# The maximum pass of an attention stage: two row tiles of the matrix array at a time, one maximum over two banks, and the maxima turned by one product and a DMA

## The chip, the cores and the metric

One Trainium2 chip, one of its cores. The metric is the device time of one launch in microseconds (us), the median of several runs. The engines are named as the profile names them: PE (matrix products; PEld its weight loads), DVE (vector), ACT (scalar), POOL (GpSimd) and SP (which issues most DMAs).

## The reference

Two layers over 1024 latent tokens and 256 context tokens of width 1024. Each layer projects the modulated stream once and splits the result into three groups of heads: six heads of a two-directional RWKV-7 recurrence, six attention heads with two key heads between them (grouped queries), and four heads of neighbourhood attention with a bias by relative position. The gated branches go through one output projection and a layer norm. The change touches the two attention branches, in the reference:

```python
def one_block(qi):                                # grouped-query heads, 128 queries at a time
    s = jnp.einsum('bqgrd,bsgd->bgrqs', qi, keys).astype(jnp.float32)
    p = jax.nn.softmax(s, axis=-1).astype(vals.dtype)
    return jnp.einsum('bgrqs,bsgd->bqgrd', p, vals)
...
s_nb = jnp.einsum('bqhd,bpqjhd->bhqpj', q_r, k_nb).astype(jnp.float32) + bias   # neighbourhood heads
s_ctx = jnp.einsum('bqhd,bchd->bhqc', q_r, k_ctx).astype(jnp.float32)
s = jnp.concatenate([s_nb.reshape(B, H, GRID_W, n_nb), s_ctx], axis=-1)
p = jax.nn.softmax(s, axis=-1).astype(v.dtype)
```

Queries and keys are 64 wide, and everything is float32. A softmax needs a value near each row's maximum taken off before the exponential; any value near it gives the same result.

## The kernel before

**Stages.** A layer is a projection, then the recurrence (`rwkv`) and the attention (`attention`), then the output projection (`out_proj`). The program is written in that order, but a scheduler sets each engine's order from a simulated time line, so the recurrence and the attention run mixed: in the profile the two share the stretches from about 560 to 1180 us (layer 0) and from about 1800 to 2390 us (layer 1). Each engine then works through its own fixed list and stops at the first instruction whose input is not there.

**Heads.** `heads` gives one piece of work after another, each of two "jobs" (two halves of its queries). A neighbourhood head (`na`) has 1024 queries and, per 128 queries, up to 384 neighbouring keys and 256 context keys. A grouped-query head (`all`) has 1024 queries on all 1280 keys. In layer 0 each of the ten heads also has a small piece for the context's own 256 queries (`ctx`). So there are 12 `all`, 8 `na` and 10 `ctx` pieces, 30 in the two layers. The loop at the end of `attention` runs the main pass of one piece (`pair_main`) with the maximum pass of the next (`pair_max`) between its steps.

**Operands.** A score is computed from float32 values split in a rounded high part and the rest (both `F32R`). `load_q` and `load_k` bring a head's queries and keys in twice, on partitions 0 to 63 and 64 to 127, and make two operands of each:

- first operand of q: high part, and rest below it; first operand of k: high part in both halves;
- second operand of q (65 rows): high part, and in row 64 the negated row maximum; second operand of k: rest, and a row of ones (L835).

Two products into one bank then give a score with its maximum taken off: L920 on the first operands, L921 on the second. ACT takes the exponential (L927), and L909 multiplies it with the values (tile `y`, in float32, which the profile shows as two passes of the array each, on 64 of its 128 columns).

**Maximum pass.** For each 128 queries, L863 multiplies the first operands into a bank `sm` (two such buffers), 512 keys at most at a time; DVE takes the maximum along the bank (L865; L867 adds the bias of a neighbourhood head as well), and L870 takes the maximum of these and negates it. When all queries of a piece are done, L876 turns each column of 128 maxima into a row by a product with the identity (one product for each 128 queries, on partition 64), and ACT copies a job's row into row 64 of the second query operand (L877). Only then can the piece's first L921 run.

In the names below `k_24741`, `q1_25626` and the like are buffers; `sm`, `st`, `y`, `ls`, `mt` are tiles in the accumulation memory: maximum pass, scores, output, sums of the softmax, turned maxima. `ch`, `kt`, `gt`, `mg` belong to the recurrence, `pso` to its output.

## Time and profile before

| what | value |
|---|---|
| three runs of the kernel | 2516.71, 2518.14, 2518.36 us (median 2518.14) |
| profiled execution, first to last instruction | 2517.7 us |
| busy: PE, DVE, POOL, ACT | 91%, 66%, 47%, 39% |
| maximum pass on PE: L863 | 436 products: 192 of 512 keys, 48 of 384, 196 of 256 |
| maxima turned: L876 | 360 passes (180 products in float32) |
| row maxima on DVE: L865, L867, L870 | 372, 64 and 180 instructions |

The profiled execution lasts as long as the runs: its span lies within 1 us of all three, so whatever its launch adds around the span is smaller than that, and a sum made against the span can be set beside the median as it is. A busy PE is not a PE at its peak: matrix products are pipelined, one begins before the other has ended, and the profile's durations of neighbours overlap. What a product costs is the distance from the end of one to the end of the next.

### The profile page before, as it was taken

What the parts mean: (1) busy time and instruction counts of PE and PEld (TensorE: products, weight loads), DVE (VectorE), ACT (ScalarE), POOL (GpSimd) and SP (SyncE); (2) the same over time, 40 slices, a digit from 0 to 9 for tenths busy, and PEclk for the clock granted to TensorE, in tenths of its full rate; (3) what the DMA queues carried; (4) which work ended last, traced back from release to release, by engine and by line L of the source; (5) the groups of instructions that cost most, each with busy time, mean ns of one, the idle gap of its engine ahead of it and who ended that gap; (6) DMA issues with size and microseconds to landing.
All of it is one profiled execution on the core that took longest, in us unless ns stands there. A gap on an engine that the chain in (4) does not pass through costs nothing. (4 is left out here: it accounts for less than half of the span.)

```text
span 2517.7 us, 56578 instructions
## 1 busy us (share of the span) xinstructions
PE 2289.5 (91%) x22008; PEld 1601.3 (64%) x22008; DVE 1669.4 (66%) x3183; ACT 979.5 (39%) x2074; POOL 1188.4 (47%) x1438
## 2 busy tenths in 40 slices
PE   6989999978898999999899999999778889999887
PEld 3878798765455554544887777887555554544387
DVE  5685524647878878665387885445478797786646
ACT  3433413333544444444233444133344444454422
POOL 4454425344555544453355465344455545544443
PEclk9999999997889999999999999999789898999999
DMA  7355325455555444441332546245645443332332
GB/s 276 117 167 169 106 80 137 101 139 115 123 117 124 104 109 102 114 140 54 104 98 95 159 143 199 87 97 138 154 105 123 101 96 97 83 80 64 112 110 95
DMA packets 448236, 298.09 MB, mean 118 GB/s; under 512 B 249600, under 2 KB 395880, under 8 KB 446944
## 3 DMA queue, kind: packets, MB, share of 16 engines
q1 hardware_dynamic: 439936, 281.71, 41.0%
q0 software_dynamic: 7392, 10.28, 1.5%
q8 instruction: 173, 2.83, 0.5%
q10 hardware_dynamic: 640, 2.49, 0.4%
q14 instruction: 95, 0.78, 0.1%
HBM read 198.37 MB, written 91.79 MB: 115 GB/s over the span
## 5 line engine op out<-in xcount | busy, mean ns | idle before, releaser
L204 PE MATMUL pj<-hlo,wh 128*128 128x512 f32 (+1 forms) x1072 | 400.7, 374 | 14.0 <-DVE hlo L480 7.9
L203 PE MATMUL pj<-hhi,wh 128*128 128x512 f32 (+1 forms) x1072 | 402.9, 377 | 9.8 <-ACT qr L348 5.9
L205 PE MATMUL pj<-hhi,wl 128*128 128x512 f32 (+1 forms) x1072 | 398.9, 373 | 0.2 <-POOL wl L169 0.2
L909 PE MATMUL y<-pt,v 128*64 128x512 f32 (+3 forms) x784 | 343.6, 570 | 0.0
L865 DVE TENSOR_REDUCE mx<-sm 128x1 f32<-128x512 f32 (+1 forms) x372 | 200.5, 555 | 85.4 <-PE sm L863 83.3
L169 POOL TENSOR_TENSOR wl<-wf,wh 128x512 fp32r<-128x512 f32 x104 | 142.9, 1378 | 205.8 <-ACT wh L168 181.8
L204 PEld LDWEIGHTS pj<-hlo,wh 128*128 128x128 f32 x1072 | 204.2, 191 | 55.3 <-DVE hlo L480 8.2
L203 PEld LDWEIGHTS pj<-hhi,wh 128*128 128x128 f32 x1072 | 203.9, 191 | 55.5 <-ACT qr L348 7.2
L927 ACT ACTIVATE pt<-st 128x512 f32<-128x512 f32 (+1 forms) x292 | 166.7, 583 | 179.4 <-PE st L921 176.9
L205 PEld LDWEIGHTS pj<-hhi,wl 128*128 128x128 f32 x1072 | 204.0, 190 | 37.2 <-issue 2.9
L863 PE MATMUL sm<-k,q 128*128 128x256 f32 (+2 forms) x436 | 167.2, 427 | 20.8 <-DVE mx L865 13.6
L920 PE MATMUL st<-q,k 128*128 128x512 f32 (+3 forms) x376 | 166.8, 447 | 18.3 <-DVE pt L929 6.2
L863 PEld LDWEIGHTS sm<-k,q 128*128 128x128 f32 x436 | 80.3, 203 | 151.8 <-DVE mx L865 41.6
L1141 PE MATMUL pj<-yh,wh 128*128 128x256 f32 x576 | 161.2, 291 | 15.9 <-ACT yh L1115 11.8
L934 POOL TENSOR_TENSOR acc<-acc,pt 128x512 f32<-128x512 f32 x80 | 107.0, 1337 | 138.1 <-ACT pt L927 137.6
L1142 PE MATMUL pj<-yl,wh 128*128 128x256 f32 x576 | 164.4, 288 | 1.0 <-POOL yl L1116 0.9
L1143 PE MATMUL pj<-yh,wl 128*128 128x256 f32 x576 | 162.8, 287 | 0.0
L921 PE MATMUL st<-q,k 65*128 65x512 f32 (+3 forms) x376 | 147.7, 396 | 1.8 <-issue 1.1
L909 PEld LDWEIGHTS y<-pt,v 128*64 128x64 f32 x784 | 72.0, 143 | 104.8 <-issue 94.1
L616 DVE TENSOR_TENSOR G<-gt,msk 64x192 f32<-64x192 f32 (+1 forms) x320 | 110.3, 345 | 39.4 <-PE gt L611 28.0
L920 PEld LDWEIGHTS st<-q,k 128*128 128x128 f32 x376 | 74.8, 200 | 93.8 <-ACT pt L927 28.1
L699 POOL MEMSET X<- 32x192 f32 x320 | 81.7, 255 | 108.8 <-PE ch L742 84.5
(276 smaller groups left out, 5126.5 us busy)
## 6 DMA issues: line engine op xcount, KB each, us to landing
wf<-win SPq DMA_DIRECT2D x104, 256.0 KB
wm<-wmod SPq DMA_DIRECT2D x32, 512.0 KB
yf<-yg_d SPq DMA_DIRECT2D x72, 128.0 KB
wt<-wm SPq DMA_DIRECT2D x8, 1024.0 KB
gate_d<-o SPq DMA_DIRECT2D x32, 256.0 KB
wf<-wout SPq DMA_DIRECT2D x16, 512.0 KB
ldkk<-rw_d SPq DMA_DIRECT2D x40, 192.0 KB
ldkd<-rw_d SPq DMA_DIRECT2D x40, 192.0 KB
```

Of the source, the lines that this page charges most:

```text
L203: nc.tensor.matmul(out=ps[:, :n], lhsT=wh, rhs=hhi[:, k, t0:t0 + n], start=(k == 0), stop=False)
L204: nc.tensor.matmul(out=ps[:, :n], lhsT=wh, rhs=hlo[:, k, t0:t0 + n], start=False, stop=False)
L205: nc.tensor.matmul(out=ps[:, :n], lhsT=wl, rhs=hhi[:, k, t0:t0 + n], start=False, stop=(k == KT - 1))
L863: nc.tensor.matmul(out=sp_[:, :o], lhsT=q[0][:, qc:qc + 128], rhs=k[0][:, c0:c0 + o], start=True, stop=True)
L865: nc.vector.tensor_reduce(out=mx[:, n_:n_ + 1], in_=sp_[:, :o], op=ALU.max, axis=AX.X)
L909: nc.tensor.matmul(out=o, lhsT=v[:, t, :], rhs=p_, start=start, stop=stop and n_ >= len(mm) - 2, tile_position=(0, 64 * i))
L920: nc.tensor.matmul(out=o, lhsT=k[0][:, 128 * t:128 * t + 128], rhs=q[0][:, qa:qb], start=True, stop=False)
L921: nc.tensor.matmul(out=o, lhsT=k[1][0:65, 128 * t:128 * t + 128], rhs=q[1][0:65, qa:qb], start=False, stop=True)
L927: nc.scalar.activation(out=pt[:, :w], in_=sp_[:, :w], func=AF.Exp)
L1141: nc.tensor.matmul(out=p_, lhsT=wh[m][:, k], rhs=yh, start=(x_ == 0), stop=False)
L1142: nc.tensor.matmul(out=p_, lhsT=wh[m][:, k], rhs=yl, start=False, stop=False)
L1143: nc.tensor.matmul(out=p_, lhsT=wl[m][:, k], rhs=yh, start=False, stop=(x_ == KT - 1))
```

## The change

What it does, part by part:

- **Operands laid out anew.** The first query operand holds the high part in both halves, the first key operand the high part with the rest below it. The second operands are four buffers of 128 partitions that stay for the whole layer (`kq0` to `kq3`): in q, the negated maximum in row 0, zeros, and the rest in rows 64 to 127; in k, a row of ones, zeros, and the high part in rows 64 to 127. Zeros and ones are written once a layer, by six DVE instructions. The second score product is 128 rows deep in place of 65.
- **Two row tiles at a time.** A product of the maximum pass is now 64 rows deep (high part by high part). Two of them are issued one behind the other, one on rows 0 to 63 of the array and one on rows 64 to 127, into two banks of one tile `sm`. That tile has one buffer, in a pool of its own, where there were two buffers of one bank.
- **One maximum over two banks.** For an `all` piece DVE takes the maximum over 1024 keys at once, and over the last 256 keys of two groups of queries at once; for a `ctx` piece over both groups. A neighbourhood head keeps its two reductions for each 128 queries. The last maximum, with the negation, is one instruction for a whole piece.
- **Turned by one product, flattened by a DMA.** One product with the identity turns all of a piece's maxima (up to 8 rows of 128), ACT copies them to a small tile `mr`, and a DMA that POOL issues lays the rows behind one another in row 0 of the second query operand.
- `load_k` has one more ACT copy, `load_q` one less.

The core of the diff:

```diff
+        psm = es.enter_context(tc.tile_pool(name=f"psm{l}", bufs=1, space=PSUM, side="right"))
...
+        kq2 = [ap1.tile([128, T], F32R, tag=f"kq{i}", name=f"kq{i}") for i in range(4)]
+        zsrc = ident[0:64, 0:64]
...
+        for z in kq2:
+            nc.vector.tensor_scalar(out=z[0:64, :], in0=zsrc[:, :].unsqueeze(2).to_broadcast([64, 64, 20]), scalar1=0.0, scalar2=None, op0=ALU.mult)
+        for z in kq2[0:2]:
+            nc.vector.tensor_scalar(out=z[0:1, :], in0=zsrc[0:1, :].unsqueeze(2).to_broadcast([1, 64, 20]), scalar1=0.0, scalar2=1.0, op0=ALU.mult, op1=ALU.add)
...
         def load_k(h):
...
-            k2 = ap2.tile([65, T], F32R, tag="k2", name="k2")
+            k2 = kq2[nkq[0] % 2]
             nc.scalar.copy(k1, sg_)
-            nc.gpsimd.tensor_tensor(out=k2[0:64, :], in0=sg_[0:64, :], in1=k1[0:64, :], op=ALU.subtract)
-            nc.vector.tensor_scalar(out=k2[64:65, :], in0=sg_[64:65, :], scalar1=0.0, scalar2=1.0, op0=ALU.mult, op1=ALU.add)
+            nc.scalar.copy(k2[64:128, :], k1[64:128, :])
+            nc.gpsimd.tensor_tensor(out=k1[64:128, :], in0=sg_[64:128, :], in1=k1[64:128, :], op=ALU.subtract)
...
         def load_q(h):
...
             nc.scalar.copy(q1[:, lo:], sg_[:, lo:])
-            nc.scalar.copy(q2[0:64, lo:], q1[0:64, lo:])
-            nc.gpsimd.tensor_tensor(out=q1[64:128, lo:], in0=sg_[64:128, lo:], in1=q1[64:128, lo:], op=ALU.subtract)
+            nc.gpsimd.tensor_tensor(out=q2[64:128, lo:], in0=sg_[64:128, lo:], in1=q1[64:128, lo:], op=ALU.subtract)
...
         def pair_max(q, k, jobs, nq, bias):
...
+            def both(*pcs):
+                sp_ = psm.tile([128, 2, 512], F32, tag="sm", name="sm")
+                for i, (qc, c0, o) in enumerate(pcs):
+                    h = slice(64 * i, 64 * i + 64)
+                    nc.tensor.matmul(out=sp_[:, i, :o], lhsT=q[0][h, qc:qc + 128], rhs=k[i][h, c0:c0 + o], start=True, stop=True, tile_position=(64 * i, 0))
+                return sp_
...
+                for u in range(0, n, 2):
+                    for x_ in range(2):
+                        top(mx[:, u + x_, 0:1], both((at[u + x_], 0, 512), (at[u + x_], 512, 512)), axis=AX.XY)
                         yield
+                    top(mx[:, u:u + 2, 1], both((at[u], 1024, TC), (at[u + 1], 1024, TC))[:, :, :TC], axis=AX.X)
+                    yield
+            nx = 1 if nq == 128 else 2
+            top(nm[:, :n], mx[:, :n, :nx], axis=AX.X, negate=True)
+            mt = psm.tile([128, 2, 512], F32, tag="sm", name="mt")
+            nc.tensor.matmul(out=mt[:n, 0, 0:128], lhsT=nm[:, :n], rhs=ident, start=True, stop=True)
+            mr = ap2.tile([8, 128], F32R, tag="mr", name="mr")
+            nc.scalar.copy(mr[:n], mt[:n, 0, 0:128])
+            nc.gpsimd.dma_start(out=q[1][0:1, at[0]:at[0] + 128 * n].rearrange("o (n t) -> o n t", t=128), in_=mr[:n])
+            yield
...
-                        nc.tensor.matmul(out=o, lhsT=k[1][0:65, 128 * t:128 * t + 128], rhs=q[1][0:65, qa:qb], start=False, stop=True)
+                        nc.tensor.matmul(out=o, lhsT=k[1][:, 128 * t:128 * t + 128], rhs=q[1][:, qa:qb], start=False, stop=True)
```

The lines have new numbers: the maximum product is L874 (was L863), the two score products are L946 and L947 (were L920 and L921), the output product L935 (was L909), the turning product L900 (was L876), the DMA L903.

The scheduler orders the new program anew. Three places show what that means; in all of them it is layer 1, and a row names line, operation, output and inputs.

First PE in the middle of a grouped-query head's main pass. Before:

```order
L909 MATMUL y_25634<-pt1_25749,v_24746 64x512
L715 MATMUL ch_17371<-rsb_22372,tt_21366 32x64 x12
L863 MATMUL sm_25758<-k1_25616,q1_25626 128x512
L920 MATMUL st_25786<-q1_25313,k1_24741 128x512
L921 MATMUL st_25786<-q2_25314,k2_24742 128x512
L909 MATMUL y_25634<-pt0_25764,v_24746 64x512
L863 MATMUL sm_25775<-k1_25616,q1_25626 128x256
L920 MATMUL st_25792<-q1_25313,k1_24741 128x512
L921 MATMUL st_25792<-q2_25314,k2_24742 128x512
L909 MATMUL y_25634<-pt1_25770,v_24746 64x512
```

The same place now:

```order
L935 MATMUL y_25158<-pt0_25269,v_24915 64x512
L874 MATMUL sm_25302<-k1_24911,q1_25152 128x512
L874 MATMUL sm_25302<-kq1_23531,q1_25152 128x512
L946 MATMUL st_25294<-q1_24920,k1_24911 128x512
L947 MATMUL st_25294<-kq3_23533,kq1_23531 128x512
L935 MATMUL y_25158<-pt1_25275,v_24915 64x512
L946 MATMUL st_25306<-q1_24920,k1_24911 128x512
L947 MATMUL st_25306<-kq3_23533,kq1_23531 128x512
L935 MATMUL y_25158<-pt0_25291,v_24915 64x512
```

The two products of a pair stand side by side and write one `sm`; before, single ones stood spread between the others. The score products keep their place, and now stand behind products of another array form.

Second, PE where one head's main pass ends and the next one's begins (`st_25916` and `st_25921` before, `st_25393` and `st_25398` now, are the new head's first two score tiles). Before, from the first turning product on:

```order
L876 MATMUL mt_25890<-c_ident_62,nm_25648 1x128 x4
L626 MATMUL kt_22429<-c_ident_62,kb_21842 128x128 x3
L876 MATMUL mt_25896<-c_ident_62,nm_25648 1x128 x4
L626 MATMUL kt_22437<-c_ident_62,kb_21876 128x128 x3
L921 MATMUL st_25916<-q2_25627,k2_25617 128x512
```

Now:

```order
L946 MATMUL st_25398<-q1_25152,k1_24911 128x512
L900 MATMUL mt_25376<-c_ident_62,nm_25172 8x128
L874 MATMUL sm_25406<-k1_24911,q1_25384 128x512
L874 MATMUL sm_25406<-kq1_23531,q1_25384 128x512
L725 MATMUL ch_16923<-X2_16950,S2_16938 64x64 x6
L725 MATMUL ch_16923<-X2_16950,S3_16939 64x64 x6
L947 MATMUL st_25393<-kq2_23532,kq1_23531 128x512
```

Eight turning products became one, and between it and the first score product that needs its result stand one pair and twelve small products.

Third, POOL at that same boundary, where there was no DMA before (L844 makes the next head's rest, L994 gates the output of the last head, L934 adds up exponentials):

```order
L844 TENSOR_TENSOR q1_26184<-stg_26181,q1_26184 64x1024
L699 MEMSET X2_17398 32x3x64 x4
L785 TENSOR_TENSOR yo_22585<-yo_22585,go_22587 128x384
L994 TENSOR_TENSOR ys_26161<-ys_26161,gtl_25910 128x512
L934 TENSOR_TENSOR acc0_26193<-pt0_26198,pt0_26217 128x512
```

Now (L855 was L844, L1020 was L994, L960 was L934):

```order
L785 TENSOR_TENSOR yo_22433<-yo_22433,go_22435 128x384
L855 TENSOR_TENSOR kq3_23533<-stg_25381,q1_25384 64x1024
L1020 TENSOR_TENSOR ys_25367<-ys_25367,gtl_25155 128x512
L903 DMA kq2_23532<-mr_25378 1x8x128
L767 TENSOR_TENSOR yo_22464<-yo_22464,yo_22465 128x384
L960 TENSOR_TENSOR acc0_25391<-pt0_25396,pt0_25413 128x512
```

The DMA that carries the maxima stands on POOL behind the next head's rest and the last head's gate.

More of the change, by code (lines that the diff above doesn't have):

```diff
@@ L852, in pair_max @@
         def pair_max(q, k, jobs, nq, bias):
+            n = 2 * nq // 128
+            at = [j["q0"] + 128 * qt for j in jobs for qt in range(nq // 128)]
             nm = ap2.tile([128, 8], F32, tag="nm", name="nm")
[L855 to L871 removed]
@@ L872, in pair_max @@
-            for i, job in enumerate(jobs):
-                q0 = job["q0"]
-                mt = pst.tile([128, 512], F32, tag="sm", name="mt", bufs=2)
-                for qt in range(nq // 128):
-                    nc.tensor.matmul(out=mt[64:65, 128 * qt:128 * qt + 128], lhsT=nm[:, 4 * i + qt:4 * i + qt + 1], rhs=ident, start=True, stop=True, tile_position=(0, 64))
-                nc.scalar.copy(q[1][64:65, q0:q0 + nq], mt[64:65, :nq])
-                yield
+            mx = ap2.tile([128, 8, 2], F32, tag="mx", name="mx")
@@ new lines, in both, with top @@
+            def both(*pcs):
[4 more added lines that the diff above has]
+                return sp_
+            def top(dst, src, **kw):
+                nc.vector.tensor_reduce(out=dst, in_=src, op=ALU.max, **kw)
@@ L880, in pair_main @@
+            yield
         def pair_main(q, k, v, jobs, nq, och, bias, end):
@@ L999, in pair_main, with job @@
             yield
-        def job(q0, steps, parts):
+        def job(q0, steps, parts=None):
             return dict(q0=q0, steps=steps, parts=parts)
-        ctx_jobs = [job(128 * i, [[(0, None, None), (1, None, None)]], lambda qt: [(0, TC, None)]) for i in range(2)]
-        all_jobs = [job(TC + 512 * i, [[(t, None, None)] for t in range(10)], lambda qt: [(0, 512, None), (512, 512, None), (1024, 256, None)]) for i in range(2)]
+        ctx_jobs = [job(128 * i, [[(0, None, None), (1, None, None)]]) for i in range(2)]
+        all_jobs = [job(TC + 512 * i, [[(t, None, None)] for t in range(10)]) for i in range(2)]
         def na_job(i):
@@ L1057, in attention @@
                 mg = pair_max(q, k, jobs, nq, bias)
-                npc = sum(len(j["parts"](t)) for j in jobs for t in range(nq // 128)) + 2
+                npc = 2 if nq == 128 else 9 if bias else 13
             if cur is not None:
```

34 lines of the change are left out of this document (16 added, 18 removed).

## Prediction

> **What bounds the kernel.** I read the page's busy shares first, then the two mixed stretches (recurrence and attention) by windows, then PE's time line inside them, and the waits last.
>
> ```profile
> core 0: us, PE busy (x) PEld busy (x) DVE busy (x) ACT busy (x) POOL busy (x), PEclk, DMA share, GB/s
> 560.00:860.00 300.00, 259.03 (x3718) 158.04 (x3706) 241.79 (x637) 137.84 (x338) 149.22 (x210) 0.87 0.52 119
> 860.00:1175.00 315.00, 303.84 (x3312) 152.41 (x3310) 227.51 (x498) 147.20 (x329) 159.79 (x177) 0.96 0.41 110
> 1860.00:2160.00 300.00, 263.01 (x3742) 151.73 (x3740) 245.59 (x623) 127.36 (x302) 152.45 (x211) 0.91 0.45 105
> 2160.00:2385.00 225.00, 215.83 (x2223) 102.25 (x2221) 166.16 (x333) 111.79 (x235) 115.33 (x121) 1.00 0.32 86
> ```
>
> The first and third rows hold mainly the neighbourhood heads, the other two the grouped-query heads. In the latter PE is busy 96% of the time and DVE 72 to 74%: PE is the bound there. In the former PE has 86 to 88%, DVE 81 to 82%, and the granted clock is lower (0.87 and 0.91): two engines in turn, with waits. So PE time taken out counts nearly whole in the grouped-query windows and in part in the others.
>
> What a product costs on PE stands in the time line of a grouped-query head:
>
> ```profile
> start us, us, engine line op out<-in xcount [idle before <-releaser]
> 1080.58 0.40 PE L921 MATMUL st<-q,k 65*128 65x512 f32 x1
> 1080.91 1.07 PE L909 MATMUL y<-pt,v 128*64 128x512 f32 x2
> 1081.91 0.73 PE L863 MATMUL sm<-k,q 128*128 128x512 f32 x2
> 1082.49 0.39 PE L920 MATMUL st<-q,k 128*128 128x512 f32 x1
> 1082.72 0.40 PE L921 MATMUL st<-q,k 65*128 65x512 f32 x1
> ...
> 1085.41 1.07 PE L909 MATMUL y<-pt,v 128*64 128x512 f32 x2
> 1086.42 0.50 PE L920 MATMUL st<-q,k 128*128 128x512 f32 x1
> ```
>
> From end to end: the two L863 end at 1082.64, 0.66 after the y before them; L920 then ends 0.24 later, L921 0.24 after that. But the L920 that follows a y directly ends 0.44 after it (1086.48 to 1086.92). So a 512-wide product costs 0.24 us behind one of the same array form, and 0.44 where the form changes (64 columns to 128): 0.20 more, about one weight load, which is then not hidden. The pair of L863 is 0.44 and 0.24, less a rounding.
>
> **The change, part by part.**
>
> *Turning the maxima.*
>
> ```profile
> 2241.74 1.03 PE L876 MATMUL mt<-c_ident,nm 128*1 128x128 f32 x8
> L876 PE MATMUL mt<-c_ident,nm x360: 270/273/422, 570.3 to 2348.1; 128*1 128x128 f32 x180
> L877 ACT CAST q<-mt x60: 251/576/578, 574.2 to 2348.7; 1x512 fp32r<-1x512 f32 x40, 1x128 fp32r<-1x128 f32 x20
> L843 ACT CAST q<-q 64x1280 fp32r<-64x1280 f32 x10 | 12.5, 1254 | 0.1
> ```
>
> Eight passes take 1.03 us, one alone 0.27, so each costs (1.03 - 0.27) / 7 = 0.11. 360 passes become 60 (one product in two passes for each of 30 pieces): 300 x 0.11 = 33 us off PE. On ACT 40 copies of 0.58 and 20 of 0.25 become 30 short ones, some 20 us less, and the copies added and dropped by the loaders (12 more, 20 less) take 8 x 1.25 = 10 us off. ACT has half its time free: nothing for the sum.
>
> *Row tiles.* There are 218 pairs: 96 of 512 wide, 122 whose hidden half is 256 wide. If the two of a pair lie over each other, the second costs nothing: 96 x 0.24 + 122 x 0.12 (half of 0.24, an estimate) = 38 us off PE. If they take turns, nothing is won, and the second weight load may stand open as well, 218 x 0.20 = 44 us lost. No product of this form is in the trace. Nearest is the recurrence's product on 32 by 32 tiles:
>
> ```profile
> 2245.09 0.38 PEld L715 LDWEIGHTS ch<-rsb,tt 32*32 32x32 f32 x24 [0.36 <-issue]
> 2245.09 0.53 PE L715 MATMUL ch<-rsb,tt 32*32 32x64 f32 x22
> L863 PEld LDWEIGHTS sm<-k,q 128*128 128x128 f32 x436 | 80.3, 203 | 151.8 <-DVE mx L865 41.6 <-issue 26.8 <-DVE tmp L644 8.1
> ```
>
> 24 weight loads within 0.38 us and 22 products within 0.53: on different tiles both lie over one another. I take full overlap less 0.01 us for each pair: 36 off.
>
> *Array forms.* By the order of the built programs, the first score product of a tile stands behind another form 175 times before and 257 times now, since a maximum product beside it used to have its own form. The other groups change little in sum. 82 x 0.20 = 16 us more on PE; the bounds are 0 (half an array beside a whole one counts as no change) and 20 (the maximum products themselves find another form ahead of them 20 times more often).
>
> The Trainium skill (TensorEngine Tiling (Array Packing), Key Properties) says that changing the tiling mode, not just the tile, drains the engine. The trace agrees as far as the change from 64 to 128 columns goes (0.44 against 0.24). By that rule the 16 us stand, without it 0.
>
> *DVE.*
>
> ```profile
> L865 DVE TENSOR_REDUCE mx<-sm 128x1 f32<-128x512 f32 x192 | 129.2, 684 | 53.3 <-PE sm L863 52.3
> L865 DVE TENSOR_REDUCE mx<-sm 128x1 f32<-128x256 f32 x180 | 75.0, 418 | 32.1 <-PE sm L863 31.1
> L870 DVE TENSOR_REDUCE nm<-mx 128x1 f32<-128x3 f32 x96 | 14.2, 148 | 0.8
> L835 DVE TENSOR_SCALAR k<-stg 1x1280 fp32r<-1x1280 f32 x12 | 18.4, 1535 | 5.5 <-DMA stg<-k_d 5.1
> ```
>
> 256 more elements cost 684 - 418 = 266 ns, so one maximum over 1024 takes 684 + 532 = 1216 against 2 x 684: 0.15 less, 96 times; two of 256 in one save the same, 58 times. 23 us. 180 final maxima become 30: 150 x 0.148 = 22 us. The 12 rows of ones go and 12 fills come, eight of them 64 rows high; nearest is L835 itself: nothing, between 10 less and 10 more. In all 45 us of DVE, worth nothing where PE has 96%.
>
> *The way of the maxima to the scores.* After the turning product: ACT copy 0.25 in place of 0.58, then POOL's DMA.
>
> ```profile
> L561 POOL DMA_DIRECT2D zs<-zs_d x40: 531/560/722, 357.7 to 2167.0; - x40
> DMA to landing us min/median/max: 2.0/2.2/8.6
> L934 POOL TENSOR_TENSOR acc<-acc,pt 128x512 f32<-128x512 f32 x80 | 107.0, 1337 | 138.1 <-ACT pt L927 137.6
> L921 PE MATMUL st<-q,k 65*128 65x512 f32 x272 | 113.7, 418 | 1.8 <-issue 1.1 <-ACT q L877 0.5
> ```
>
> The nearest DMA from POOL is this one, a tile of the recurrence: 0.56 us of POOL, 2.2 us to the landing. Behind a sum on POOL (1.34 us, third row) it waits half of that, 0.7, as an estimate. So L947 may run about 3.5 us after the turning product, where L921 needed the copy's 0.58 and the hand-overs, about 1. In layer 0 the order puts 3 us or more of other products there at all pieces but the first. In layer 1 I count, with the prices above, 0.7 to 1.3 us of cover at five of the ten heads, 3 to 4.4 at the rest. PE stands some 2.5 us at six places: 15 us. Bounds: 0 (covered), 30 x 2.5 = 75. POOL gets 30 x 0.56 = 17 us at 47% busy; queued behind a DMA that waits are the sums of the exponentials, with three buffers of slack: nothing.
>
> *One buffer for sm.* The next pair may not start before DVE has read both banks, 1.2 us and its queue.
>
> ```profile
> PE sm L863 <- DVE mx L865: 13.6, 16, 3.2
> L863 PE MATMUL sm<-k,q 128*128 128x256 f32 x196 | 70.9, 370 | 14.6 <-DVE mx L865 8.6 <-POOL q L844 4.8 <-DVE mx L867 0.8
> ```
>
> PE already waits 13.6 us for these, with two buffers. In the new order most pairs stand 2 us or more apart, and some 26 of 247 closer than DVE needs; I take 10 us more, bounds 0 and 30. On the other side the maximum no longer needs POOL's subtraction (the last row's 4.8 us): 3 off.
>
> *Sum.* PE: -33 -36 +16 = -53. Two thirds of it (35) falls to the grouped-query heads (288 of 436 products, 192 of 360 passes) and is taken whole; of the other 18 half, 9, since DVE is as near there. Of DVE's 45 about 10 lie in the neighbourhood windows; half, 5. -35 -9 -5 -3 +15 +10 = -27 us on a span of 2517.7, 0.4 below the median: 2491.
>
> **The rivals.**
>
> *Slower: the waits grow and bring the clock down.* After a lull PE gets half its clock:
>
> ```profile
> 685.20:691.20 6.00, 2.82 (x43) 2.27 (x43) 5.94 (x3) 3.05 (x8) 5.91 (x5) 1.00 0.67 171
> 691.20:701.40 10.20, 9.97 (x55) 6.47 (x56) 7.12 (x18) 1.73 (x5) 3.46 (x4) 0.50 0.33 88
> ```
>
> Six us at less than half busy were followed by 10.2 us at clock 0.50. If the DMA's way is open at 20 of the 30 pieces for 2.5 us, and each lull costs as much again in half clock, that is 100 us in place of 15: about 2575 at the worst, 2540 with half of it. It decides the sign from 52 us of such waits on (27 + 25). For it: the order leaves under 1.3 us of cover at half the heads of layer 1. Against it: PE hardly idles at these places now (0.5 us in all, in the L921 row), and in layer 0 the maxima are ready long before.
>
> *Slower: the row tiles take turns.* The 36 us go and up to 44 come; at half of that, 2491 + 36 + 22 = 2549, or 2527 if the loads stay hidden. Against it stands the L715 row.
>
> By the Trainium skill (TensorE: Matmul & The Clock Gate, "Packing small matmuls — row/col tiling") products on different rows run concurrently, about 4 ns apart. No row of this case shows 64-row tiles; by that page the term would be 37 us, not 0.
>
> *No change: the recurrence's chain ends last.* If its steps, PE to DVE to ACT and back, set the end, less PE work only leaves PE idle. Then the waits and the gains cancel: 2515. For it, the recurrence's output products start as late as 2401.6, past the end of the attention's own:
>
> ```profile
> L780 PEld LDWEIGHTS pso<-c_ident,yo x54: 137/141/144, 638.9 to 2401.6; 128*128 128x128 f32 x54
> ```
>
> Against it, PE is busy 96% in the last part, and the new order ends the recurrence earlier in the attention than the old.
>
> *More: everything counts.* If half of DVE's 45 us count and no wait comes: 2518 - 53 - 22 = 2443; a middle value is 2465.
>
> **How the numbers follow.** The forecast (2478 to 2508 by itself) gets 0.48, more than that 0.14, no change 0.13, growing waits 0.15, tiles in turn 0.10. A measurement can tell 0.2%, 5 us. Faster: 0.48 + 0.14 and a rest of the slower cases' milder ends, 0.63; within 0.2%: 0.13; slower 0.24. The range leaves out the far ends of the slower cases and of "more": 2460 to 2535.
>
> **What would show it.** In the profile after: the pair's two L874 should start within some 20 ns and end together; if they start 0.2 us apart, the tile term is wrong. L900 should be 60 passes. L946 should end 0.44 us after a pair, not 0.24. L865's heirs should take about 1.22 us on 1024 elements. The wait of L947 for the DMA into `kq2` or `kq3` should add up to 15 us, the pairs' wait for DVE's maximum to some 24; if either passes 50, or the granted clock in the last two windows falls below 0.96 and 1.00, the slower rival has won. The forecast fails if PE stays 96% busy in those windows while they don't get shorter.

## The result, and the profile after

The changed kernel takes 2582.27 us in the median (four runs, 2571.95 to 2597.68) against 2518.25: 1.0262 times as long, interval 1.0227 to 1.0297. The forecast of 2491 and its range up to 2535 are both missed, on the slow side. The profiled execution has a span of 2574.3 us against 2517.7; the mean granted clock fell from 0.949 to 0.917.

Most of the forecast's pieces are there. PE's time line in the middle of a grouped-query head of the changed kernel:

```profile
2109.50 0.50 PE L874 MATMUL sm<-k,q 64*128 64x512 f32 x1
2109.50 0.49 PE L874 MATMUL sm<-kq,q 64*128 64x512 f32 x1
2109.93 0.50 PE L946 MATMUL st<-q,k 128*128 128x512 f32 x1
2110.26 0.39 PE L947 MATMUL st<-kq,kq 128*128 128x512 f32 x1
```

The two halves of a pair begin together and end together; the score product behind them ends 0.43 us after them (2109.93 + 0.50 against 2110.00), the next one 0.22 later. (Over the 51 places where a 512-wide score product follows a pair without a gap, the median is 0.43 too.) Groups of the changed kernel (maximum, turning product, DMA, fills), the second a row of its line's own list:

```profile
L878 DVE TENSOR_REDUCE mx<-sm 128x1 f32<-128x1024 f32 x96 | 117.2, 1221 | 52.3 <-PE sm L874 51.5
L900 PE MATMUL mt<-c_ident,nm x60: 269/323/421, 590.1 to 2402.5; 128*8 128x128 f32 x40, 128*2 128x128 f32 x20
L903 POOL DMA_DIRECT2D kq<-mr x30 | 17.2, 572 | 35.2 <-ACT mr L902 32.7 <-DVE sm L774 2.3 <-issue 0.2
L834 DVE TENSOR_SCALAR kq<-c_ident 64x1280 fp32r<-64x1280 f32 x8 | 9.4, 1234 | 0.0
```

The waits of PE that the forecast named, one of the turning product, and two of the recurrence's (in total, times, longest, us), after:

```profile
PE ch L725 <- DVE X L721: 31.8, 19, 7.3
PE sm L874 <- DVE mx L878: 25.7, 15, 11.8
PE ch L715 <- ACT rsb L710: 23.2, 10, 11.8
PE mt L900 <- DVE nm L878: 18.0, 10, 4.0
PE st L947 <- DMA kq<-mr: 7.4, 8, 2.0
```

and the last three of before:

```profile
PE ch L715 <- ACT rsb L710: 14.7, 11, 3.9
PE ch L725 <- DVE X L721: 5.6, 7, 1.5
PE mt L876 <- DVE nm L870: 2.0, 3, 0.8
```

Two waits of the new parts came out as forecast (sm 25.7 for 24, the DMA 7.4 on PE and 9.6 on its weight loads for 15). Two others were not in the forecast. The turning product now waits 18.0 us for the last maximum, where it waited 2.0. And the waits of the *recurrence* grew, by 35 us for these two lines. Three single waits in layer 0 alone come to 26 us: one of 11.8 us at 588 us, to which we come back, and two of 7.1 and 7.3 us. Behind these two stand engines that waited for loads (time lines of PE, ACT and POOL):

```profile
949.85 1.26 ACT L844 CAST k<-stg 128x1280 fp32r<-128x1280 f32 x1 [8.71 <-DMA stg<-k_d]
954.99 1.55 PE L725 MATMUL ch<-X,S 128*64 128x64 f32 x24 [7.09 <-DVE X L721]
970.55 0.99 POOL L767 TENSOR_TENSOR yo<-yo 128x384 f32<-128x384 f32 x1 [8.42 <-DMA yo<-y_d]
972.64 1.55 PE L725 MATMUL ch<-X,S 128*64 128x64 f32 x24 [7.34 <-DVE X L721]
```

At the first, ACT's list holds the recurrence's copy (L721) behind the next head's keys, which had not landed; at the second, DVE's list holds its copy behind a step that needs POOL's L767, which waited for its own load.

Where the time went shows when a layer is cut at the recurrence's last product (L742, tile `ch`): up to there attention and recurrence run together, then the attention ends alone. Windows of before, layer 0 and layer 1, together and alone:

```profile
core 0: us, PE busy (x) PEld busy (x) DVE busy (x) ACT busy (x) POOL busy (x), PEclk, DMA share, GB/s
566.30:1109.40 543.10, 497.59 (x6698) 282.96 (x6698) 420.58 (x1055) 248.93 (x600) 267.07 (x359) 0.92 0.47 112
1109.40:1197.50 88.10, 86.27 (x334) 35.00 (x336) 55.28 (x90) 40.16 (x76) 39.49 (x26) 0.96 0.31 99
1823.80:2347.00 523.20, 471.39 (x6348) 261.99 (x6347) 409.29 (x1016) 233.92 (x539) 269.18 (x352) 0.93 0.38 91
2347.00:2388.30 41.30, 36.79 (x104) 11.57 (x106) 29.21 (x33) 22.68 (x38) 18.16 (x8) 0.96 0.49 156
```

and after:

```profile
574.90:1090.70 515.80, 426.27 (x6228) 248.73 (x6227) 366.19 (x872) 217.87 (x542) 259.88 (x362) 0.85 0.46 109
1090.70:1232.00 141.30, 135.60 (x548) 52.03 (x544) 76.32 (x104) 56.60 (x111) 55.88 (x42) 0.94 0.30 88
1848.70:2365.70 517.00, 436.61 (x6175) 236.76 (x6170) 377.80 (x852) 216.62 (x513) 266.45 (x357) 0.87 0.40 94
2365.70:2443.20 77.50, 68.94 (x213) 24.06 (x211) 46.60 (x59) 33.91 (x61) 35.58 (x22) 0.91 0.32 96
```

Together the two stretches became 33 us shorter (1066 to 1033), and PE, busy 92% and 90% of them before, is now busy 83% and 84%, at clock 0.85 and 0.87. The attention that did not fit in comes behind: 219 us alone in place of 129. -33 + 89 = 56 is nearly the whole difference of the spans (56.6).

The same in another cut. PE's span is its work at full clock, plus what the stretches at clock 0.50 add to it (half of the busy time that lies in them), plus idle time. All three are worked out from the records of the profile, for each kernel told of here. "Rows left" is the number of output products (L909, now L935; two passes each) that stand in PE's order behind the recurrence's last product, in layer 0 and layer 1; "together" and "alone" are the stretches above, both layers added. The ratio is that of the medians of several runs; the other columns are of the one profiled execution, which can lie some us off its median (`fill_lead`: 2538.78 for 2555.16, the most here).

| kernel | ratio to before | rows left | work | half clock | idle | together | alone | span |
|---|---|---|---|---|---|---|---|---|
| before | 1 | 44, 20 | 2184 | 105 | 228 | 1066 | 129 | 2518 |
| after | 1.0262 | 71, 36 | 2110 | 157 | 307 | 1033 | 219 | 2574 |
| pace_b | 1.0052 | 47, 20 | 2172 | 111 | 236 | 1060 | 131 | 2519 |
| late_b | 1.0148 | 44, 23 | 2189 | 116 | 240 | 1084 | 140 | 2545 |
| lead_b | 1.0078 | 32, 4 | 2184 | 102 | 248 | 1114 | 74 | 2534 |
| add_pe | 1.0269 | 43, 23 | 2219 | 125 | 236 | 1107 | 145 | 2581 |
| cut_pe | 0.9961 | 44, 20 | 2138 | 115 | 250 | 1054 | 122 | 2503 |
| dma_idle | 1.0152 | 44, 23 | 2196 | 117 | 239 | 1078 | 141 | 2552 |
| dma_only | 1.0146 | 44, 24 | 2137 | 138 | 282 | 1077 | 157 | 2557 |
| one_tile | 1.0205 | 68, 24 | 2162 | 134 | 276 | 1034 | 202 | 2572 |
| bufs1 | 1.1274 | 116, 85 | 2206 | 241 | 386 | 935 | 573 | 2833 |
| rt_only | 1.0206 | 59, 20 | 2189 | 136 | 240 | 1085 | 150 | 2565 |
| two_buf | 1.0108 | 52, 21 | 2149 | 132 | 257 | 1071 | 141 | 2538 |
| no_dma | 1.0293 | 72, 30 | 2147 | 159 | 291 | 1049 | 220 | 2597 |
| pace_a | 1.0273 | 71, 29 | 2103 | 168 | 315 | 1056 | 207 | 2586 |
| lead_a | 1.0157 | 40, 20 | 2116 | 147 | 285 | 1103 | 126 | 2548 |
| act_fill | 1.0150 | 68, 32 | 2109 | 155 | 282 | 1025 | 202 | 2547 |
| fill_lead | 1.0171 | 35, 20 | 2126 | 145 | 266 | 1103 | 115 | 2537 |
| two_fill | 1.0345 | 66, 25 | 2143 | 163 | 302 | 1086 | 192 | 2607 |
| two_fill_lead | 1.0171 | 49, 20 | 2147 | 149 | 269 | 1093 | 142 | 2564 |

PE's work did fall, by 74 us where the sum had 53. (The same PE instructions in other orders give 2172 to 2189 for the kernel before and 2103 to 2126 for the changed one, so work, too, moves by up to 20 us with the order.) Idle time rose by 79, and the half clock by 52.

### The profile page after: what moved, and what is told of

Same layout as the page of the kernel before. It is cut to its first block, busy times and chain, and to the rows that moved or that the text cites. A ratio compares the mean times of both kernels' runs of the same rounds, so it can differ in the third digit from the quotient of the medians.

```text
span 2574.3 us, 55864 instructions
## 1 busy us (share of the span) xinstructions
PE 2267.3 (88%) x21708; PEld 1576.2 (61%) x21708; DVE 1626.6 (63%) x2879; ACT 956.2 (37%) x2036; POOL 1207.5 (47%) x1468
## 5 line engine op out<-in xcount | busy, mean ns | idle before, releaser
L935 PE MATMUL y<-pt,v 128*64 128x512 f32 (+3 forms) x784 | 337.3, 571 | 3.7 <-ACT pt L956 2.6
L878 DVE TENSOR_REDUCE mx<-sm 128x1 f32<-128x1024 f32 (+2 forms) x218 | 183.8, 843 | 83.3 <-PE sm L874 81.4
L946 PE MATMUL st<-q,k 128*128 128x512 f32 (+3 forms) x376 | 178.6, 479 | 7.6 <-DVE pt L955 3.2
L960 POOL TENSOR_TENSOR acc<-acc,pt 128x512 f32<-128x512 f32 x80 | 109.1, 1363 | 105.5 <-ACT pt L953 103.9
L947 PE MATMUL st<-kq,kq 128*128 128x512 f32 (+3 forms) x376 | 146.5, 398 | 8.0 <-DMA kq<-mr 7.4
L946 PEld LDWEIGHTS st<-q,k 128*128 128x128 f32 x376 | 76.0, 203 | 118.9 <-ACT pt L953 42.3
L935 PEld LDWEIGHTS y<-pt,v 128*64 128x64 f32 x784 | 70.8, 144 | 108.6 <-issue 93.8
L874 PE MATMUL sm<-k,q 64*128 64x512 f32 (+2 forms) x218 | 107.2, 492 | 29.0 <-DVE mx L878 25.7
L960 DVE TENSOR_TENSOR acc<-acc,pt 128x512 f32<-128x512 f32 x112 | 97.6, 874 | 48.1 <-ACT pt L953 47.4
L874 PEld LDWEIGHTS sm<-k,q 64*128 64x128 f32 x218 | 44.3, 203 | 134.3 <-DVE mx L878 36.2
```

The source lines that it names most:

```text
L874: nc.tensor.matmul(out=sp_[:, i, :o], lhsT=q[0][h, qc:qc + 128], rhs=k[i][h, c0:c0 + o], start=True, stop=True, tile_position=(64 * i, 0))
L878: nc.vector.tensor_reduce(out=dst, in_=src, op=ALU.max, **kw)
L935: nc.tensor.matmul(out=o, lhsT=v[:, t, :], rhs=p_, start=start, stop=stop and n_ >= len(mm) - 2, tile_position=(0, 64 * i))
L946: nc.tensor.matmul(out=o, lhsT=k[0][:, 128 * t:128 * t + 128], rhs=q[0][:, qa:qb], start=True, stop=False)
L947: nc.tensor.matmul(out=o, lhsT=k[1][:, 128 * t:128 * t + 128], rhs=q[1][:, qa:qb], start=False, stop=True)
L960: eng.tensor_tensor(out=acc[i][:, :w], in0=sums[i][:, :w], in1=pt[:, :w], op=ALU.add)
```

## Experiments: one part alone, one part undone

Theory 1 is that the single two-bank tile costs the loss, by tying the attention to DVE pair by pair and letting it fall behind the recurrence. Its rivals: the way of the maxima by DMA (2), row tiles and operand layout (3). Three came in as runs asked for them: that any new order of the program costs waits (4), that PE's time is no bound any more (5), and that the fills at a layer's start push the recurrence back (6).

**The single tile without the rest** (`one_tile`, on the kernel before) and **with the rest but undone** (`two_buf`, on the changed kernel). In `one_tile` the turning products write the single tile too, and the last maximum is taken once for a piece; in `two_buf` every bank gets its own maximum again:

```diff
 # one_tile: products 128 rows deep and the turning as before
-sp_ = pst.tile([128, 512], F32, tag="sm", name="sm", bufs=2)
+psm = es.enter_context(tc.tile_pool(name=f"psm{l}", bufs=1, space=PSUM, side="right"))
+sp_ = psm.tile([128, 2, 512], F32, tag="sm", name="sm")   # two products, one maximum over both
...
 # two_buf: against the changed kernel
-sp_ = psm.tile([128, 2, 512], F32, tag="sm", name="sm")
+sp_ = [psm.tile([128, 512], F32, tag="sm", name="sm") for _ in pcs]   # two buffers, one maximum per bank
```

> The kernel before, but its maximum pass takes two products at a time into one two-bank tile with a single buffer, with one maximum over both banks; products are still 128 rows deep, operands and the turning as before. Theory 1 (single buffer): slower by much of what the change lost, 2555 to 2600, with the waits of the products for the maximum grown to 25 us or more. Theories 2 and 3 (DMA, row tiles): 2500 to 2525, as before or a little faster, since DVE does 45 us less.

Measured 1.0205 (1.0143 to 1.0267), 2571.21 us. The tile alone makes the kernel before as slow as theory 1 said, with 22 us *less* PE work; its products' wait for the maximum is no more than 15.0 us, not the 25 expected (13.6 before). The price shows elsewhere: 202 us alone for 129.

> The changed kernel, but each of the two products of a pair writes its own one-bank tile, from two buffers, and each bank gets its own maximum (so the maximum over two banks is given up: DVE does some 20 us more). Row tiles, operands, the one turning product and its DMA stay. Theory 1 (the single two-bank buffer ties PE to DVE pair by pair, lets the order put the attention behind the recurrence, and costs nearly all of the loss): most of the 64 us come back, 2500 to 2535, and the recurrence's last product is no longer followed by a longer attention-only end. Theory 2 (the DMA at the piece boundaries): 2570 to 2590, as the changed kernel. Theory 3 (row tiles and operand layout: array forms, the extra copy, the fills at the start): 2570 to 2600.

Measured 1.0108 (1.0076 to 1.0140), 2548.87 us: 39 us back by the ratios, the attention alone down to 141 us, but not all of the loss. That is above theory 1's range and below the other two. The undoing is not clean: with two tiles the scheduler puts other products between the halves, and only 127 of 218 pairs begin within 40 ns of each other (211 in the changed kernel); 39 us of PE work come back.

**The maxima's way, done alone and undone** (`dma_only` on before, `no_dma` on after):

```diff
 # dma_only
-for qt in range(nq // 128):
-    nc.tensor.matmul(out=mt[64:65, 128 * qt:128 * qt + 128], lhsT=nm[:, 4 * i + qt:4 * i + qt + 1], ...)
-nc.scalar.copy(q[1][64:65, q0:q0 + nq], mt[64:65, :nq])
+nc.tensor.matmul(out=mt[:n, 0:128], lhsT=nm[:, :n], rhs=ident, start=True, stop=True)
+nc.scalar.copy(mr[:n], mt[:n, 0:128])
+nc.gpsimd.dma_start(out=q[1][64:65, p0:p0 + 128 * n].rearrange("o (n t) -> o n t", t=128), in_=mr[:n])
...
 # no_dma: the changed kernel, turned product by product again, into row 0
```

> The kernel before, but with one turning product for a whole piece and the DMA that lays the rows into row 64 of the second query operand; all else as before. Theory 1 (single buffer): 33 us of PE go, some 15 us of waits come: 2490 to 2515. Theory 2 (DMA): slower, 2550 or more. Theory 3: as theory 1.

Measured 1.0146 (1.0094 to 1.0199), 2558.22 us, with 47 us less PE work. This is theory 2's range; theories 1 and 3 had 2490 to 2515.

> The changed kernel, but the maxima are turned product by product, as before, and ACT copies them straight into row 0 of the second query operand; no DMA from POOL. PE does 300 short passes more (about 33 us by the 0.11 us that one costs). Theory 1 (single buffer): 2575 to 2615, the passes come on top. Theory 2 (the way by DMA costs the loss): under 2550, since the 17 us of waits for the DMA and the clock lost behind them go. Theory 3: as theory 1.

Measured 1.0293 (1.0243 to 1.0344), 2594.7 us: the range of theories 1 and 3, far above theory 2's; taking the DMA out of the changed kernel wins nothing (37 us of PE work come back, 17 us of idle time go). So the DMA seems dear in one program and cheap in the other. The visible waits are small in `dma_only` too (PE's weight loads and PE):

```profile
PEld st L922 <- DMA q<-mr: 8.9, 4, 5.9
PE st L922 <- DMA q<-mr: 8.1, 3, 5.6
```

**Row tiles alone** (`rt_only`: `two_buf` and `no_dma` together).

> The row tiles and their operand layout alone: two one-bank buffers with one maximum per bank, and the maxima turned product by product and copied by ACT as before. No instruction of the maximum pass is dearer than before and PE has some 20 us less to do (36 less for the pairs, 16 more for the array forms). Theory 3 (row tiles and layout cost by themselves): 2540 or more, with waits at the products themselves. If only the single buffer and the way by DMA cost: 2495 to 2520. Theory 4 (every new order that the scheduler makes costs PE idle time in waits on the recurrence's chains, whatever is changed): 2525 to 2560, with PE's busy time down and its idle time up.

Measured 1.0206 (1.0179 to 1.0234), 2565.95 us, and PE's work did not fall at all (110 of 218 pairs begin together, the other products run by themselves). The time is theory 3's, but not its sign: the products wait 6.5 us for the maximum, less than before. Theory 4's range ended at 2560, and idle time is up by 11 us with the work not down. Still, every part alone is slower than before, the single tile or not; that spoke for theory 4, and its test needs kernels in which nothing but the order differs.

## Experiments: nothing but the order

```diff
 # pace_b (before) and pace_a (after); late_b has npc * i
-while mg is not None and done < npc * (i + 1) // nit:
+while mg is not None and done < npc * (i + 2) // nit:
...
 # lead_a; lead_b has (3000, 2600)
-attention(l)
+with tc.high_priority(offset=(3000, 2300)[l]):
+    attention(l)
```

> The kernel before with not one instruction changed: only the place in the written program at which the next piece's maximum steps are put between the main steps of the piece in hand is one main step earlier. The scheduler then makes another order. Theory 4 (the order before is a lucky one, and others cost waits): 2530 to 2560. If the order's details don't matter: 2510 to 2525.

> As the kernel before, not one instruction changed, with the maximum steps one main step later instead. Theory 4: 2525 to 2560. If the order's details don't matter: 2510 to 2525.

Measured 1.0052 (1.0027 to 1.0076) and 1.0148 (1.0120 to 1.0176): 13 and 37 us with the same instructions. `pace_b` falls between its two expectations, `late_b` in theory 4's. The order before is a favourable one.

> The changed kernel, not one instruction changed, with the next piece's maximum steps one main step earlier. If its loss comes from the single buffer as such (theory 1): within 15 us of the changed kernel, 2570 to 2595. If it comes from the order that the scheduler happened to make (theory 4): it moves by 10 to 40 us in either direction, 2540 to 2610.

Measured 1.0273 (1.0253 to 1.0292), 2581.27 us: as the changed kernel, which is theory 1's case and misses the step that theory 4 asked for; 71 rows are left in layer 0 as there.

> The changed kernel, not one instruction changed: the scheduler is told a higher priority for the attention, so that when the recurrence's last step is issued 40 and 20 of the output product's rows are left in layer 0 and 1 (44 and 20 before, 71 and 36 in the changed kernel). Theory 1, now as a theory of the order (a pair takes all the banks of the maximum pass, so the attention falls behind the recurrence and ends alone): some 20 us come back in each layer, 2530 to 2550. If the lag is only a symptom: 2565 to 2595.

Measured 1.0157 (1.0124 to 1.0190), 2556.0 us: 26 us back by the medians, short of the 32 to 52 expected. The time alone fell from 219 to 126 us, but the stretch together grew by 70. Its 60 rows left are fewer than the 64 before, and it still takes 39 us more than before: the attention's lag does not account for these.

> The kernel before, not one instruction changed, with a higher priority for the attention: 32 and 4 rows left after the recurrence's last step, in place of 44 and 20. If a shorter end of the attention alone is what makes a layer short: 2500 to 2515. If the order before is only a lucky one among many (theory 4): 2525 to 2560.

Measured 1.0078 (1.0052 to 1.0103), 2536.62 us, in theory 4's range. The end alone is 74 us for 129, and no gain: now the recurrence is late. PE's time line at the end of layer 1 in this kernel:

```profile
2385.97 0.66 PE L978 MATMUL tb<-c_ident,rb 128*128 128x128 f32 x4 [1.04 <-ACT rb L970]
2397.93 0.88 PE L780 MATMUL pso<-c_ident,yo 128*128 128x128 f32 x3 [11.30 <-issue]
2414.92 1.22 PE L1141 MATMUL pj<-yh,wh 128*128 128x256 f32 x4 [16.12 <-ACT yh L1115]
```

PE idles 27 us in two pieces, and the chain that ended last runs there through the steps of the recurrence's own output (L773 to L786, then its transfer `yg_d`). A lag of zero is not the optimum either.

## Experiments: is PE's time worth anything, and the three suspects

```diff
 # add_pe
-for qt in range(nq // 128):
+for qt in 2 * list(range(nq // 128)):
...
 # cut_pe: leaves out part of the output products
+wd = 384 if nq == 512 and not first else nq
-mm.append((x_, i, t, y[64 * i:64 * i + 64, :nq], pt[:, nq * x_:nq * x_ + nq], ...))
+mm.append((x_, i, t, y[64 * i:64 * i + 64, :wd], pt[:, nq * x_:nq * x_ + wd], ...))
...
 # bufs1 (the tile sm, and mt with it)
-sp_ = pst.tile([128, 512], F32, tag="sm", name="sm", bufs=2)
+sp_ = pst.tile([128, 512], F32, tag="sm", name="sm", bufs=1)
...
 # dma_idle: the old way stays, and beside it
+nc.tensor.matmul(out=m8[:n, 0:128], lhsT=nm[:, :n], rhs=ident, start=True, stop=True)
+nc.scalar.copy(mr[:n], m8[:n, 0:128])
+nc.gpsimd.dma_start(out=ro[:n], in_=mr[:n])
...
 # act_fill, against the changed kernel (the rows of ones alike)
-nc.vector.tensor_scalar(out=z[0:64, :], in0=zsrc[:, :].unsqueeze(2).to_broadcast([64, 64, 20]), scalar1=0.0, ...)
+nc.scalar.activation(out=z[0:64, :], in_=zsrc[:, :].unsqueeze(2).to_broadcast([64, 64, 20]), func=AF.Identity, scale=0.0)
```

> The kernel before with every turning product issued twice: 360 short passes more, about 40 us of PE by the 0.11 us of one, and nothing else on any engine. If PE's time is the bound, as the prediction had it: 2550 to 2560. Theory 5 (PE's time in the mixed stretches is not the bound: what it saves turns into idle time, and into half clock behind that, and what it gets in addition fills idle time): 2515 to 2540 with the idle time lower.

> The kernel before with the output product of the grouped-query heads and of the context keys left out for 128 of 512 queries at every step but a head's first: some 45 us of PE less and nothing else changed on any engine; those queries get no full sums. If PE's time is the bound: 2465 to 2485. Theory 5: 2500 to 2540, with the idle time up by most of what the products lost. Theory 4 adds up to 25 us to either.

Measured 1.0269 (1.0241 to 1.0298) and 0.9961 (0.9938 to 0.9983). By the spans +63 for 35 us of work more, -15 for 47 us less. `add_pe` lies above both its ranges; `cut_pe` lies in theory 5's, and also in the other one with theory 4's 25 us on it. Both are some 30 us above what PE's work says, and `late_b` is 28 above before. Between the two, 78 us of time stand against 81 us of work, 0.96 of a microsecond for each. That speaks against theory 5, but it is one difference of two kernels, each with an order of its own; with 20 us for the order the 0.96 could be 0.7 or 1.2.

> The kernel before with one buffer of one bank for the maximum pass in place of two; not one instruction changed. In the order that the scheduler makes, 116 and 85 rows of the output product are left after the recurrence's last step, in place of 44 and 20. Theory 1 (too few buffers put the attention behind the recurrence, which then ends alone): 2600 to 2680, with the waits of the maximum products for DVE still under 60 us. If a buffer costs only the waits seen at the products: 2540 to 2570.

Measured 1.1274 (1.1231 to 1.1316), 2833.64 us: 314 us for one buffer less, far over the range given. Its windows, cut as above:

```profile
568.80:1046.80 478.00, 381.22 (x6042) 243.36 (x6042) 332.83 (x889) 191.64 (x490) 219.08 (x324) 0.81 0.45 107
1046.80:1368.70 321.90, 285.26 (x990) 112.93 (x992) 140.13 (x257) 99.71 (x187) 86.13 (x61) 0.82 0.19 57
1995.10:2452.30 457.20, 367.08 (x5913) 228.57 (x5909) 331.69 (x864) 185.48 (x455) 217.40 (x316) 0.84 0.41 98
2452.30:2703.70 251.40, 212.68 (x590) 78.01 (x588) 109.11 (x188) 78.22 (x133) 70.28 (x48) 0.82 0.13 38
```

and its first row of PE's waits:

```profile
PE sm L863 <- DVE mx L865: 93.0, 103, 5.1
```

The wait at the products is 93 us, 79 more than before (over the 60 expected), a quarter of the loss. Here the instructions are the same, but with a buffer less the scheduler's order is another too. The recurrence is done after 478 and 457 us and the attention then runs 573 us by itself: 444 us more alone buy only 131 us less together, so in this kernel a microsecond of attention pushed out of the common stretch cost 0.70.

> The kernel before, which in addition turns all maxima of a piece by one product, copies them on ACT and sends them with a DMA from POOL to a tile that nobody reads: the way by DMA as load on PE (8 us), ACT, POOL and the queues, but with nothing that waits for it. A new order has cost 20 to 35 us in the five kernels that had little else. If the load of the DMAs on POOL is what made the kernel with the DMA slow: 2570 or more. If it is the waiting for it: 2540 to 2565.

Measured 1.0152 (1.0113 to 1.0191), 2552.49 us, 33 us more, 11 of them PE's work; the other 22 lie within what a new order costs by itself. So the load of the DMAs needs no price of its own, as expected if only the waiting counts. `dma_only` has as many DMAs and 59 us less PE work, and takes as long: its idle time and half clock are 43 and 21 us higher, in waits and in the order that goes with them.

> The changed kernel with the six fills of a layer (zeros and ones of the second operands) done by ACT in place of DVE, where they stood 7.7 us in a row ahead of the recurrence's L565, L575 and L616 in layer 0. Theory 6 (the fills push the recurrence's start back; its loads then come behind the attention's and PE stands 11.8 us at the start of each layer, with half clock behind it): 2550 to 2568, and the long gap at 576 us is gone. If they are hidden, as the prediction had it: 2572 to 2595.

Measured 1.0150 (1.0112 to 1.0187), 2549.81 us: 28 us better than the changed kernel by the ratios, at the fast end of theory 6's range. What the fills did at the start of layer 0 in the changed kernel (SP's, DVE's and PE's time lines):

```profile
543.33 5.98 DVE L834 TENSOR_SCALAR kq<-c_ident 64x1280 fp32r<-64x1280 f32 x4
553.35 0.17 DVE L575 COPY dc<-lp 128x12 f32<-128x12 f32 x1 [1.37 <-ACT lp L573]
562.91 3.05 SPq L595 DMA_DIRECT2D ls_d<-G  x2
582.36 0.37 DVE L635 COPY nn<-lin 64x256 f32<-64x256 f32 x1 [9.66 <-DMA lin<-ls_d]
587.92 0.86 PE L715 MATMUL ch<-rsb,tt 32*32 32x64 f32 x24 [11.79 <-ACT rsb L710]
```

and the same places before:

```profile
543.97 0.48 DVE L575 COPY dc<-lp 128x12 f32<-128x12 f32 x1 [1.27 <-ACT lp L573]
549.56 3.57 SPq L595 DMA_DIRECT2D ls_d<-G  x2
563.98 2.50 DVE L635 COPY nn<-lin 64x256 f32<-64x256 f32 x1 [3.89 <-DMA lin<-ls_d]
```

L575 comes 9 us later, behind fills of 6 us; the recurrence's DMA of `ls_d` then stands on SP behind the next attention loads and goes out 13 us later; `lin` is read 18 us later; and PE stands 11.8 us, with nothing of the attention ready either. But most of this stays in `act_fill`, where DVE has no fills (ACT has them, 7.3 us between 540 and 549 us):

```profile
549.72 0.42 DVE L575 COPY dc<-lp 128x12 f32<-128x12 f32 x1
560.59 1.94 SPq L595 DMA_DIRECT2D ls_d<-G  x2
576.47 0.37 DVE L635 COPY nn<-lin 64x256 f32<-64x256 f32 x1 [7.51 <-DMA lin<-ls_d]
558.58 0.86 PE L715 MATMUL ch<-rsb,tt 32*32 32x64 f32 x24 [7.96 <-ACT rsb L710]
578.67 0.86 PE L715 MATMUL ch<-rsb,tt 32*32 32x64 f32 x24 [7.28 <-ACT rsb L710]
```

`ls_d` still goes out 11 us later than before and `lin` is read 12 us later, and in place of one gap of 11.8 us PE has two, of 8.0 and 7.3. From 540 to 600 us PE idles 27 us, for 29 in the changed kernel and 25 before. The recurrence is 2 to 6 us ahead of the changed kernel at these three places. So the fills on DVE are not shown to be what holds the start of the layer, and most of the 28 us lies elsewhere.

> The last kernel, and the attention at the higher priority that brought the changed kernel down to 2556. If the start of a layer and the lag of the attention are two separate causes: 2525 to 2545. If they are one: 2550 to 2560.

Measured 1.0171 (1.0131 to 1.0210), 2555.16 us: no gain over `act_fill`, though the time alone fell from 202 to 115 us; together grew by 78. The two do not add, as the second expectation had it. So the last two kernels put the fills on ACT and took the single tile out (`two_buf`), at two lags.

> The two things that brought the changed kernel most, together: a pair in two one-bank tiles of two buffers with a maximum for each bank (that kernel took 1.0108 of the time before), and the fills on ACT (28 us won on the changed kernel). In this order 66 and 25 rows of the output product are left after the recurrence's last step, against 52 and 21 with the fills on DVE. If the fills are a price of their own: 27 - 28, about 2520, and with 15 to 20 us for the longer lag 2530 to 2540. If the gain of the fills' move was the luck of one order: 2540 to 2570.

> The last kernel with a higher priority for the attention, not one instruction changed: 49 and 20 rows left in place of 66 and 25. If the lag decides: 10 to 20 us below the last kernel, 2505 to 2525, which may beat the kernel before. If it is a symptom, or the order's luck is larger: no clear step, 2525 to 2560.

Measured 1.0345 (1.0300 to 1.0389) and 1.0171 (1.0128 to 1.0214): 2607.17 and 2564.84 us. The first is the slowest kernel but `bufs1`, above all of its expectations (2570 at the most). The same move of the fills that won 28 us on the changed kernel lost 60 on `two_buf`, by the ratios; so the 28 us of `act_fill` are no price of the fills, and theory 6 is not borne out. Between the two only the priority differs: 50 us less alone and 42 us less time, more than the 10 to 20 expected of the lag, though the time itself lies above both ranges. Neither beats the kernel before, and no version here with the whole work in it does.

## Why the prediction was wrong, point by point

- **Turning the maxima, right.** 60 passes of L900. Against `no_dma`, the changed kernel has 37 us less PE work; the term was 33.
- **Row tiles, right.** A pair costs what one product costs: by the medians both end 0.43 us after a product of another form. The Trainium skill (TensorE: Matmul & The Clock Gate, "Packing small matmuls — row/col tiling") has products on different rows about 4 ns apart; by the trace 211 of the 218 pairs begin within 0.01 us.
- **Array forms, right in kind.** L946 ends 0.43 us after a pair, where 0.44 was forecast. In sum it was too dark: PE's work fell by 74, not 53. `one_tile` lost 22 us of it with no row tiles and no fewer passes, so products that stand in pairs may win back about what the forms cost. That is argued, not isolated, and 21 us are near what an order alone moves.
- **DVE, right.** 1626.6 us for 1669.4, 43 less for 45, and 1221 ns for one maximum where 1216 was worked out. The fills, taken for nothing, stood ahead of the recurrence's first steps; what they cost there is not shown, since moving them to ACT won 28 us on one version and lost 60 on another. The last maximum, now one for a whole piece, was counted only as a gain: the turning product's wait for it, 18.0 us for 2.0, had no term.
- **The way of the maxima, right as a wait, and open as a price.** Seen at L947: 7.4 us and 9.6 us. Beyond that it cost much in `dma_only` and nothing in the changed kernel against `no_dma`; as load it shows no cost beyond that of a new order (`dma_idle`).
- **One buffer for sm, the step that failed, together with the next.** It was sized by the wait at the product, 10 us more with bounds 0 and 30, and the product does wait about that (25.7 for 13.6). But a pair takes both banks that the maximum pass has, so no second pair can be under way. What the term left out is where the attention then ends: more of it stands behind the recurrence's last product and runs when nothing else fills PE (219 us alone for 129). `one_tile` shows 52 us with less PE work, and `bufs1` 314 us for one buffer less. That the lag itself costs time is seen where the priority alone differs: 26 us come back in `lead_a`, 42 in `two_fill_lead`. (`fill_lead` against `act_fill` wins none, and `lead_b` loses 20: the lag is not the only thing an order sets.) How much of the 52 is the tile and how much its order stays open: `rt_only` lost as much without the single tile, and `late_b` 37 without any edit. One rival was not run by itself: a maximum over two banks holds DVE for 1.22 us where one over a bank takes 0.68, and `one_tile` and `two_buf` change that along with the buffer. It is not the main source of the recurrence's longer waits, as L725 waits 20.0 and 25.2 us in `two_buf` and `rt_only` too, whose maxima cover one bank.
- **The order, at nothing in the sum.** The prediction took the new order's array forms and its covers for the DMA from the listing, but left the rest of the order at nothing. With not one instruction changed it cost 13, 20 and 37 us on the kernel before, and about 30 more than PE's work says in `add_pe` and `cut_pe`. The forecast of 27 us gained was of this size. Over the kernels of the table without `bufs1`, the span rises by 1.07 us for each row left and by 0.18 us for each microsecond of PE work, with 20 us of scatter (least squares, 19 kernels; standard errors 0.3 and 0.2, and less than half of the variance accounted for). By that the 43 rows that the change adds would make 46 of its 57 us; but `lead_a`, which takes the rows away again, gets only 26 back. Nor is the 0.18 a price of PE's time, against the 0.96 above: the kernels with the least PE work are those that carry the change's other costs.
- **The rivals.** The slower one had the right chain (waits, then half clock) at the wrong place: it looked for the waits at the DMA. "The recurrence's chain ends last" was given as the no-change case: the common stretch, which by the way it is cut ends with the recurrence, shrank only by 33 us where PE's work fell by 74; but there the prediction did not ask where attention that falls behind would go. The mark it set for the slower case, a clock under 0.96 and 1.00 in the windows of the grouped-query heads, was met, as the same four windows show:

```profile
560.00:860.00 300.00, 231.28 (x3732) 148.67 (x3731) 220.00 (x573) 128.27 (x319) 155.75 (x227) 0.79 0.53 118
860.00:1175.00 315.00, 282.39 (x3142) 139.26 (x3146) 209.32 (x385) 131.29 (x302) 159.18 (x176) 0.91 0.41 110
1860.00:2160.00 300.00, 242.34 (x3756) 143.10 (x3756) 231.72 (x581) 123.76 (x299) 157.83 (x231) 0.82 0.45 103
2160.00:2385.00 225.00, 205.90 (x2298) 94.54 (x2296) 156.77 (x278) 100.39 (x225) 114.47 (x128) 0.95 0.35 89
```

The clock there is 0.91 and 0.95; its other mark, a wait over 50 us for the DMA or at the pairs, was not. In the other two windows, where the prediction counted on gains, PE fell from 86 and 88% busy to 77 and 81%, and the clock to 0.79 and 0.82. (By its own terms the milder end of this rival comes to about 2530, not 2540.)

What stays open: how the 64 us divide. The parts do not add up (single tile 52, way by DMA 37, row tiles 52, each alone on the kernel before), since each brings an order of its own, worth up to some 40 us either way. A run of the changed instructions in the old order would tell; it was not tried.

## What to carry to other kernels

Where two strands share the engines and one is a serial chain, price a buffer by the progress of the strand that fills the gaps, and not only by the wait at the instruction: count in the order how much of the filler is left when the chain ends, and hold that against the kernel before. Where a scheduler makes the order, time the unchanged kernel in two or three other orders first: their spread is the least that an edit must win, and one favourable order is hard to beat. Don't carry a gain over from one version to the next without timing it again: the same move of six fills won 28 us here and lost 60 there.

## What the runs showed of the hardware that was not expected

- More idle time came with more half clock than the forecast had: 79 and 52 us more. The stretches at clock 0.50 went from 37 of 7.0 us on average to 48 of 9.0 us; with one buffer (`bufs1`) there are 62 of 10.2 us, 634 us in all, and the attention alone has clock 0.82 though PE is busy 85 to 89% of it; over the whole run its maximum products wait 103 times, 0.9 us each.
- The Trainium skill (TensorEngine Tiling (Array Packing), "Gotcha 1: PSUM Pressure") has different row tiles write to different banks; no run here put them into one. With a bank for each of its products, a second pair would have needed two banks more.
- The same instructions in another order took from 3 to 42 us more or less (seven pairs of kernels), up to 1.6% of the kernel.
